# State-space outputs with swapped matmul operands, wider weight conversions and later transposes in a streaming encoder step

## The chip, the core and the metric

The kernel runs on one core of a Trainium2 chip. The metric is the device time in microseconds (us) of one execution, median over runs.

## What is computed

One layer of a hybrid encoder over 2048 new frames of one stream (16 tiles of 128 tokens) and 16 new frames of eight running streams (one more tile, number 16). All data are float32.

```python
h = _rms_norm(x, norm_gain)
u, g_s, q, k, v, g_a = jnp.split(h @ w_in, SPLITS, axis=-1)   # six groups of 512
y_s = S5(u)            # 32 groups of 16 channels, a 64-dim complex diagonal state each, scanned over positions
#   y = gelu(Re(C h) + D u);  z_val, z_gate = split(y @ w_glu);  y_s = z_val * sigmoid(z_gate)
y_a = BandAttn(q, k, v)   # 8 heads of 64, own chunk of 64 frames and the 8 before
out = x + concat[y_s * silu(g_s), y_a * silu(g_a)] @ w_out
```

## The kernel before

**Foreground and background.** The program is a fixed order of instructions that two generators write together. The foreground (`inproj`, `glu`, `outproj`) writes projections; after each step it yields a cost, and the background (`s5`, `decode`, `attention`) is given that cost times a ratio and writes its own instructions in between. A step is one k of a projection: three matmuls of 512 columns in `mm3` (high part by high weights L189, high by low weights L190, low by high weights L191). There are 1224 steps: three passes of the input projection (u and k; v and q; ga and gs) over 17 tiles, order 16, 0, 1, ..., 15, with 16 steps a tile; the GLU with 8 steps a tile; the output projection with 16. Each engine runs its instructions in that order, and SP issues nearly all DMAs in that order too. `defer(n, fn)` writes something n steps later. While weight conversions are due (`self.busy`, L1509) the ratio is 0, and the background gets nothing.

**Weights.** `load_w` (L136) loads a chunk of 128 x 512 into one of five raw buffers. `conv_w` (L142) splits it into a high part on ScalarE (L155) and a low part on VectorE (L156), 16 buffers each, and writes the load of chunk n + 5 two steps later (at once during the start). At the last tile of a pass `due` (L394) lays the next pass's 16 conversions (8 for the GLU) into the coming steps.

**Transposes of k and q.** `ev_norm` (L269) evacuates a k or q tile on ScalarE into `zs`, sums squares on VectorE (L279), takes the power on POOL (L281), scales `zs` on VectorE eight steps later (L284), and 14 steps later `turn` (L291) makes four TensorE transposes (L294), evacuates them as high (L303) and low parts (L304) and writes two stores.

**State space.** `s5` first prepares tables, then works through 8 batches of 4 channel groups. Time is cut in 272 columns (chunks of 8 tokens): 256 of the prompt, 16 of the samples. Per batch `u` is loaded, permuted and transposed into `UT` (L722), multiplied into `v` (`step_b1`, L771, 272 columns), rotated and scanned on VectorE, and gives the states `HP`. `build_e` (L698) copies a small table into `T` with eight DMAs. `step_c` (L834) makes the outputs in three blocks of 128, 128 and 16 columns, with the columns' data as the stationary operand (L842, L843; L849, L852), and GELUs them on ScalarE; `step_y` (L859) stores each block to `y_d`, token by token, in pieces of 256 bytes. The scan stage runs beside passes 1 and 2.

**GLU.** `glu_load` (L1334) loads a tile of `y`, `glu_tr` (L1339) transposes it with four TensorE instructions (L1344) into PSUM, and ScalarE (L1347) and VectorE (L1348) make the high and low parts that the GLU's matmuls use six steps later.

**Start.** Weights and the first two tiles are loaded in turn; 16 conversions are made, and `dma_h(2)` (L370) issues the third tile's `xraw` load after them.

## Time and profile before

| | us |
|---|---|
| median of 3 runs | 1225.95 |
| lowest, highest of them | 1225.14, 1464.7 |
| the profiled execution, its time | 1226.13 |
| its span in the profile | 1224.3 |
| TensorE, VectorE, ScalarE, POOL busy | 1193.0, 742.6, 597.7, 366.6 |

A row of the timeline gives start, duration, engine, line, operation, output<-inputs, shapes and count, and in brackets the engine's idle time before it with what ended it. Matmuls are pipelined: durations overlap, and the distance from start to start is the price.

### The profile page before, as it was taken

The page shows a single profiled execution, that of the slowest core. Times are in us where ns is not written, and L with a number is a line of the kernel's source. Part 1 is how long each engine was busy: PE and PEld are TensorE (multiplying, and loading weights), DVE is VectorE, ACT ScalarE, POOL GpSimd, SP SyncE. Part 2 cuts the span into 40 slices and gives each one's busy share as a digit, 9 for nine tenths or more (in the row PEclk, how much of TensorE's full clock was granted, in tenths as well). Part 3 has the DMA queues.
Part 4 walks back from the last instruction along what each step waited for, and adds up shares of the span by engine and source line. Part 5 has one row for each costly group of instructions (what it writes and reads, how often), then busy time and mean ns, then how long its engine had stood idle before and what let it go on. Part 6 is the DMA issues. An engine that isn't in the chain of part 4 may idle for free.

```text
span 1224.3 us, 18936 instructions
## 1 busy us (share of the span) xinstructions
PE 1193.0 (97%) x6687; PEld 983.1 (80%) x6687; DVE 742.6 (61%) x1391; ACT 597.7 (49%) x1159; POOL 366.6 (30%) x455
## 2 busy tenths in 40 slices
PE   8999999899999998999999999999999999999998
PEld 5788888777788876887777878788888888888876
DVE  5324556868999988985444456565565555555511
ACT  6434446266666656553232346565654555455410
POOL 2433242557767735540000011111211121121120
PEclk9999999999999998999999999999999999999999
DMA  8876556655545567433895688897877777767243
GB/s 252 262 250 181 155 177 202 195 142 129 149 123 151 135 195 214 110 93 88 270 382 171 204 247 245 255 265 205 217 221 215 206 240 241 196 205 225 73 136 107
DMA packets 190119, 236.58 MB, mean 193 GB/s; under 512 B 58136, under 2 KB 122656, under 8 KB 189000
## 3 DMA queue, kind: packets, MB, share of 16 engines
q1 hardware_dynamic: 189016, 232.15, 64.2%
q0 software_dynamic: 864, 3.21, 0.8%
q8 instruction: 53, 0.87, 0.3%
q14 instruction: 42, 0.34, 0.1%
q10 hardware_dynamic: 144, 0.00, 0.0%
HBM read 169.48 MB, written 67.80 MB: 194 GB/s over the span
## 4 chain that ended last, share of the span: by engine, by line
PE 78%; DMA 6%; DVE 6%; POOL 3%; ACT 3%; issue 2%; SPq 1%; DVEq 0%; ACTq 0%; POOLq 0%
PE z L189 19%; PE z L191 18%; PE z L190 18%; PE o L1218 6%; PE pt L1200 5%; PE s L1170 5%; DMA wraw<-in_w_in_dram 3%; PE pt L294 1%; PE o L1057 1%; PE y L843 1%; SPq L701 1%; PE y L842 1%; PE v L771 1%; ACT whi L155 1%; PE s L1015 1%
## 5 line engine op out<-in xcount | busy, mean ns | idle before, releaser
L189 PE MATMUL z<-whi,hhi 128*128 128x512 f32 x816 | 339.2, 416 | 1.4 <-ACT whi L155 0.7
L190 PE MATMUL z<-wlo,hhi 128*128 128x512 f32 x816 | 321.3, 394 | 3.3 <-DVE wlo L156 3.1
L191 PE MATMUL z<-whi,hlo 128*128 128x512 f32 x816 | 320.7, 393 | 0.5 <-DVE hlo L231 0.5
L189 PEld LDWEIGHTS z<-whi,hhi 128*128 128x128 f32 x816 | 154.1, 189 | 38.9 <-issue 5.1
L190 PEld LDWEIGHTS z<-wlo,hhi 128*128 128x128 f32 x816 | 154.5, 189 | 36.5 <-DVE wlo L156 8.0
L191 PEld LDWEIGHTS z<-whi,hlo 128*128 128x128 f32 x816 | 154.0, 189 | 34.3 <-DVE hlo L231 1.0
L1207 ACT ACTIVATE pth<-pt 128x640 fp32r<-128x640 f32 (+4 forms) x128 | 81.7, 639 | 129.3 <-PE pt L1200 89.4
L1208 DVE TENSOR_TENSOR ptl<-pt,pth 128x640 fp32r<-128x640 f32 (+4 forms) x128 | 94.6, 739 | 60.6 <-ACT pth L1207 59.7
L189 PE MATMUL z<-whi,mh 128*128 128x512 f32 x272 | 113.7, 418 | 0.0
L1115 POOL MEMSET bias<- 64x64 f32 x32 | 4.7, 146 | 363.5 <-DMA bias<-tl_d 250.0
L1189 ACT ACTIVATE sn<-sn,mn 128x640 f32<-128x640 f32 (+4 forms) x128 | 96.9, 757 | 29.5 <-DVE mn L1180 29.4
L191 PE MATMUL z<-whi,ml 128*128 128x512 f32 x272 | 107.1, 394 | 1.3 <-POOL ml L1415 1.3
L190 PE MATMUL z<-wlo,mh 128*128 128x512 f32 x272 | 106.7, 392 | 0.0
L1180 DVE CUSTOM_DVE_ANT_0 sn<-s,bias 128x640 f32<-128x640 f32 (+4 forms) x128 | 93.3, 729 | 11.4 <-PE s L1170 10.4
L1170 PE MATMUL s<-ks,q 128*128 128x320 f32 (+1 forms) x448 | 87.4, 311 | 0.0
L1200 PE MATMUL pt<-ident,sn 128*128 128x128 f32 x560 | 83.0, 274 | 3.9 <-DVE ptl L1208 3.1
L1170 PEld LDWEIGHTS s<-ks,q 128*128 128x128 f32 x448 | 74.7, 188 | 11.1 <-DVE mn L1180 1.2
L1200 PEld LDWEIGHTS pt<-ident,sn 128*128 128x128 f32 x560 | 64.9, 140 | 22.5 <-ACT sn L1189 10.0
L231 DVE TENSOR_TENSOR hlo<-xraw,hhi 128x1024 fp32r<-128x1024 f32 x49 | 60.9, 1242 | 20.7 <-ACT hhi L228 20.6
L280 POOL TENSOR_SCALAR s<-s 128x8 f32<-128x8 f32 x34 | 15.9, 468 | 182.9 <-DVE s L279 182.3
L1228 DVE TENSOR_TENSOR ot<-o,tmp 64x512 f32<-64x512 f32 x32 | 22.0, 689 | 74.5 <-ACT tmp L1226 74.5
L191 PEld LDWEIGHTS z<-whi,ml 128*128 128x128 f32 x272 | 51.0, 188 | 13.2 <-POOL ml L1415 1.7
(268 smaller groups left out, 2171.3 us busy)
## 6 DMA issues: line engine op xcount, KB each, us to landing
xraw<-in_xT_dram SPq DMA_DIRECT2D x49, 512.0 KB, 4.5
q<-qt_d SPq DMA_DIRECT2D x64, 256.0 KB, 8.6
ks<-kt_d SPq DMA_DIRECT2D x28, 512.0 KB, 5.6
vhl<-vp_d SPq DMA_DIRECT2D x28, 512.0 KB, 6.7
wraw<-in_w_in_dram SPq DMA_DIRECT2D x48, 256.0 KB, 4.5
bias<-tl_d SPq DMA_DIRECT2D x32, 320.0 KB, 6.3
mt<-mt_d SPq DMA_DIRECT2D x17, 512.0 KB, 7.4
x<-in_x_dram SPq DMA_DIRECT2D x34, 256.0 KB, 5.8
```

What stands on the lines that cost most here:

```text
L189: mm(z, a, whi, start=first, stop=False)
L190: mm(z, a, wlo, start=False, stop=False)
L191: mm(z, b, whi, start=False, stop=last)
L231: nc.vector.tensor_sub(lo, raw, fv(hi))
L1170: nc.tensor.matmul(ps_s[:, bank, 0:wp], Q[n, x2][:, s, 128 * a:128 * a + 128], KS[n][:, s, c0:c0 + wp], start=(x2 == 0), stop=(x2 == 1))
L1180: nc.vector.tensor_tensor_reduce(out=o, in0=i0, in1=i1, scale=1.0, scalar=3e38, op0=OP.add, op1=OP.min, accum_out=mn)
L1189: nc.scalar.activation(out=sn[:, 0:w], in_=sn[:, 0:w], func=AF.Exp, scale=-1.0, bias=mn, accum_out=SUM[n][:, a, s:s + 1])
L1200: nc.tensor.transpose(t[:, k], pr[:, 128 * k:128 * k + 128], self.ident)
L1207: nc.scalar.activation(out=h, in_=t[:, 0:w], func=AF.Copy)
L1208: post.append(lambda: nc.vector.tensor_tensor(out=l, in0=t[:, 0:w], in1=fv(h), op=OP.subtract))
L1218: nc.tensor.matmul(o[:, a0:a1], VB[n][:, j, s, :], t[:, 3 * a0 + j + a0:4 * (a1 - 1) + j + 1:4], start=(y == 0 and j == 4), stop=(y == 1 a ...
L1228: post.append(lambda: nc.vector.tensor_tensor(out=ot[mine], in0=o[mine], in1=tmp[mine], op=OP.add))
```

## The change

The state-space outputs are computed with the tables as the stationary operand and the data as the moving one, one group of 272 columns at a time, so that they come out with channels on partitions; the sample's columns move from the end to the front. They are stored in that form by eight DMAs a batch, in pieces of 16 elements (64 bytes). The GLU then reads its operand already transposed, with rows of `w_glu` loaded in the matching order, and its TensorE transposes go; `glu_conv` only splits into high and low parts. At the changes of pass, conversions start at step 2 instead of 4 and are 1.6 steps apart instead of 1.25 (into the GLU still 1.25). The last tile's `turn` of k and q, and tile 16's of q, come six steps later. In the start, the five raw weights of the next pass are loaded at steps 40 to 80 instead of at once, and `dma_h(2)` comes before the last four conversions instead of after them. The first `build_c` comes after one more pause.

```diff
-        self.y_d = d.tile([NT * 128, 512], F32, name="y_d")
+        self.y_d = d.tile([4, CH, 8, NT, 128], F32, name="y_d")
...
-        self.identr = c.tile([128, 128], F32R, name="ident")
-        self.ident = fv(self.identr)
-        nc.vector.tensor_scalar(self.identr, ip, 0.0, None, op0=OP.is_equal)
+        self.ident = c.tile([128, 128], F32, name="ident")
+        nc.vector.tensor_scalar(self.ident, ip, 0.0, None, op0=OP.is_equal)
...
-            self.chunks += [((3, f, k), I["w_glu"][128 * k:128 * k + 128, 512 * f:512 * f + 512], None) for k in range(4)]
+            self.chunks += [((3, f, k), I["w_glu"][128 * k:128 * k + 128, 512 * f:512 * f + 512]
+                             .rearrange("(g h) c -> h g c", h=CH), None) for k in range(4)]
...
         if self.step:
             self.defer(self.T_LW, lambda: self.load_w(n + self.NR))
+        elif n + self.NR < 16:
+            self.load_w(n + self.NR)
         else:
-            self.load_w(n + self.NR)
+            self.defer(40 + 10 * (n + self.NR - 16), lambda: self.load_w(n + self.NR))
...
-            self.defer(self.T_TURN, turn)
+            self.defer(self.T_TURN + (6 if t == 15 or (g, t) == ("q", 16) else 0), turn)
...
             for _ in range(4):
                 self.conv_w()
-        dma_h(2)
+            if j == 0:
+                dma_h(2)
...
-                    self.due(self.step + 4, 1.25, 16 if ps < 2 else 8)
+                    self.due(self.step + 2, 1.6 if ps < 2 else 1.25, 16 if ps < 2 else 8)
...
-                            self.glu_tr(TILES[0])
+                            self.glu_conv(TILES[0])
...
         BLK = [(0, 128), (128, 128), (256, 16)]
+        COL = [16, 144, 0]
...
-            nc.scalar.activation(out=UT[b][:, :, c0:c0 + n], in_=p[:, :, 0:n], func=AF.Copy)
+            nc.scalar.activation(out=UT[b][:, :, COL[i]:COL[i] + n], in_=p[:, :, 0:n], func=AF.Copy)
...
-        def step_c(b, i):
-            c0, n = BLK[i]
-            p = ps.tile([128, GB, 128], F32, tag="y", name="y", bufs=2)
-            y = mp.tile([128, L, GB * CH], F32, tag="y", name="y")
...
-                for g in range(GB):
-                    nc.tensor.matmul(p[0:n, g], UT[b][:, g, c0:c0 + n], Tm[b % 2][:, g], start=True, stop=False)
-                    nc.tensor.matmul(p[0:n, g], HP[b][:, g, c0:c0 + n], ca[g], start=False, stop=True)
-                nc.scalar.activation(out=yg, in_=p[0:n].rearrange("p g (j h) -> p g j h", j=L), func=AF.Gelu_apprx_tanh)
...
+        def step_c(b, g):
+            if g == 0:
+                YS[b] = mp.tile([128, GB, 272], F32, tag="y", name="y", bufs=1)
+            p = ps.tile([128, 272], F32, tag="y", name="y", bufs=2)
+            nc.tensor.matmul(p, Tm[b % 2][:, g], UT[b][:, g], start=True, stop=False)
+            nc.tensor.matmul(p, CA[b][:, g, 1:9].rearrange("p j h -> p (j h)"), HP[b][:, g, 0:272],
+                             start=False, stop=True)
+            nc.scalar.activation(out=YS[b][:, g], in_=p, func=AF.Gelu_apprx_tanh)
...
-        def step_y(b, i):
-            c0, n = BLK[i]
-            y = YS.pop((b, i))
-            nc.sync.dma_start(y4[c0:c0 + n, :, b * GB * CH:(b + 1) * GB * CH], y[0:n])
+        def step_y(b):
+            y = YS.pop(b)
+            o0 = (b // 2) * CH * 8 * NT * 128 + (b % 2) * 4 * NT * 128
+            for j in range(L):
+                nc.sync.dma_start(ap_of(self.y_d, o0 + 16 * j, [[8 * NT * 128, CH], [128, GB * NT], [1, 16]]),
+                                  y[16 * j:16 * j + 16].rearrange("p g (t c) -> p (g t) c", c=16))
...
             if n == 0:
+                yield SL
                 build_c(0)
...
-                if b and 1 <= sl < 4:
-                    step_y(b - 1, sl - 1)
+                if b and sl == 3:
+                    step_y(b - 1)
...
-                if b and sl < 3:
-                    step_c(b - 1, sl)
+                if b:
+                    for g in ((0,), (1,), (2, 3), (), (), ())[sl]:
+                        step_c(b - 1, g)
...
-        for i in range(3):
-            step_c(NBATCH - 1, i)
-            yield 1740
-            step_y(NBATCH - 1, i)
+        for g in range(GB):
+            step_c(NBATCH - 1, g)
+            yield 1300
+        step_y(NBATCH - 1)
...
-        self.nc.sync.dma_start(y, self.y_d[128 * t:128 * t + 128])
+        self.nc.sync.dma_start(y.rearrange("p (k x) -> p k x", k=4),
+                               self.y_d[:, :, :, (t + 1) % NT].rearrange("k h g x -> (h g) k x"))
...
-    def glu_tr(self, t):
+    def glu_conv(self, t):
         nc = self.nc
-        y = self.GY.pop(t)
-        pt = self.pst.tile([128, 4, 128], F32, tag="tr", name="ty")
-        for k in range(4):
-            nc.tensor.transpose(rv(pt[:, k]), rv(y[:, 128 * k:128 * k + 128]), self.identr)
+        y = self.GY.pop(t).rearrange("p (k j c) -> p k c j", k=4, j=L)
         hi = self.hp.tile([128, 8, 128], F32R, tag="hhi", name="yh")
         lo = self.hp.tile([128, 8, 128], F32R, tag="hlo", name="yl")
-        nc.scalar.activation(out=hi[:, 0:4], in_=pt, func=AF.Copy)
-        self.defer(1, lambda: nc.vector.tensor_tensor(out=lo[:, 0:4], in0=pt, in1=fv(hi[:, 0:4]), op=OP.subtract))
+        h4, l4 = (v[:, 0:4].rearrange("p k (c j) -> p k c j", j=L) for v in (hi, lo))
+        nc.scalar.activation(out=h4, in_=y, func=AF.Copy)
+        self.defer(1, lambda: nc.vector.tensor_tensor(out=l4, in0=y, in1=fv(h4), op=OP.subtract))
...
-                            self.glu_tr(TILES[i + 1])
-                            yield 430
+                            self.glu_conv(TILES[i + 1])
```

## Rows read from the trace of the kernel before

**Rows 1.** The page's head: busy time, share and instructions by engine.

```profile
PE 1193.0 (97%) x6687; PEld 983.1 (80%) x6687; DVE 742.6 (61%) x1391; ACT 597.7 (49%) x1159; POOL 366.6 (30%) x455
```

**Rows 2.** Timeline of TensorE at foreground's pace: start, duration, engine, line.

```profile
443.46 0.40 PE L190 MATMUL z<-wlo,hhi 128*128 128x512 f32 x1
...
453.22 0.39 PE L191 MATMUL z<-whi,hlo 128*128 128x512 f32 x1
```

**Rows 3.** By stretch: length, busy PE, PEld, DVE, ACT, POOL, clock, DMA share, GB/s.

```profile
210.00:220.00 10.00, 7.58 (x33) 5.78 (x32) 8.04 (x13) 5.10 (x8) 4.41 (x3) 0.96 0.79 237
220.00:230.00 10.00, 10.00 (x40) 8.06 (x39) 9.76 (x26) 3.10 (x5) 2.85 (x3) 0.87 0.81 253
470.00:480.00 10.00, 7.65 (x37) 5.40 (x37) 9.65 (x15) 7.13 (x18) 8.22 (x11) 0.66 0.77 242
257.00:443.00 186.00, 184.10 (x1017) 149.07 (x1017) 168.63 (x286) 114.40 (x256) 128.92 (x144) 1.00 0.52 137
```

**Rows 4.** Timeline of TensorE: output blocks of 128 and 16 columns, and L771.

```profile
298.60 0.38 PE L842 MATMUL y<-T,UT 128*128 128x128 f32 x2
...
300.62 0.39 PE L190 MATMUL z<-wlo,hhi 128*128 128x512 f32 x1
...
304.40 0.41 PE L849 MATMUL y<-T,UT 128*16 128x128 f32 x8
...
305.29 0.40 PE L190 MATMUL z<-wlo,hhi 128*128 128x512 f32 x1
...
406.50 0.62 PE L771 MATMUL v<-UT,VB 128*128 128x272 f32 x2
...
407.18 0.39 PE L190 MATMUL z<-wlo,hhi 128*128 128x512 f32 x1
```

**Rows 5.** Timeline of TensorE: GLU's transposes, once alone, once waiting.

```profile
701.93 0.46 PE L1344 MATMUL ty<-ident,y 128*128 128x128 f32 x4
...
702.53 0.40 PE L190 MATMUL z<-wlo,hhi 128*128 128x512 f32 x1
...
707.92 0.51 PE L1344 MATMUL ty<-ident,y 128*128 128x128 f32 x4 [1.35 <-DMA y<-y_d]
```

**Rows 6.** Timeline of TensorE at the change from pass 0 to 1.

```profile
218.73 0.69 PE L294 MATMUL pt<-ident,zs 128*128 128x128 f32 x4 [2.17 <-DVE zs L284]
```

**Rows 7.** Timelines of TensorE, VectorE and ScalarE at the change from 1 to 2.

```profile
472.84 1.09 PE L294 MATMUL pt<-ident,zs 128*128 128x128 f32 x4 [2.35 <-DVE zs L284]
...
468.95 2.71 DVE L156 SCALAR_TENSOR_TENSOR wlo<-wraw,gain,whi 128x512 fp32r<-128x512 f32 x3
...
457.16 2.79 ACT L155 ACTIVATE whi<-wraw,gain 128x512 fp32r<-128x512 f32 x4 [6.24 <-DMA wraw<-in_w_in_dram]
```

**Rows 8.** Timeline of TensorE in the start and at the scan's start.

```profile
35.72 0.50 PE L191 MATMUL z<-whi,hlo 128*128 128x512 f32 x1 [0.53 <-DVE hlo L231]
...
250.51 0.41 PE L686 MATMUL pk<-CA,X 128*16 128x128 f32 x8 [1.96 <-ACT UT L734]
```

**Rows 9.** DMA issues: transfer, queue, count, KB each, median us to landing.

```profile
xraw<-in_xT_dram SPq DMA_DIRECT2D x49, 512.0 KB, 4.5
...
wraw<-in_w_in_dram SPq DMA_DIRECT2D x48, 256.0 KB, 4.5
...
qbd<-qsd SPq DMA_DIRECT2D x2, 128.0 KB, 5.4
```

**Rows 10.** Groups by line: busy us, mean ns, idle us before and releaser.

```profile
L228 ACT ACTIVATE hhi<-xraw 128x1024 fp32r<-128x1024 f32 x49 | 51.8, 1056 | 4.9 <-DMA xraw<-in_xT_dram 4.9
...
L719 ACT ACTIVATE P<-U 128x512 f32<-128x512 f32 (+1 forms) x24 | 15.0, 625 | 0.1
```

**Rows 11.** Timeline of SP: eight issues in a row of T's copies.

```profile
436.28 6.17 SPq L701 DMA_DIRECT2D T<-kr  x8
```

**Rows 12.** Instructions on `qsd`: issue ns min/median/max, first and last start.

```profile
L982 SPq DMA_DIRECT2D qbd<-qsd x2: 584/2044/3503, 589.1 to 589.7; - x2
```

**Rows 13.** Instructions on `xraw`, 257 to 577: issue ns, first and last start.

```profile
L214 SPq DMA_DIRECT2D xraw<-in_xT_dram x21: 327/339/953, 267.4 to 568.4; - x21
```

More of the change, by code (lines that the diff above doesn't have):

```diff
@@ L33, in fv @@
     return ap.bitcast(F32)
-def rv(ap):
-    return ap.bitcast(F32R)
 def ap_of(t, offset, pat):
@@ L703, in s5 @@
         u4 = self.u_d.rearrange("(c j) e -> c j e", j=L)
-        y4 = self.y_d.rearrange("(c j) e -> c j e", j=L)
         BLK = [(0, 128), (128, 128), (256, 16)]
+        COL = [16, 144, 0]
         U, P, UT, HP = {}, {}, {}, {}
@@ L726, in step_a @@
                 HP[b] = mp.tile([128, GB, 273], F32, tag="HP", name="HP")
-                nc.vector.memset(HP[b][:, :, 0:1], 0.0)
-                nc.vector.tensor_copy(HP[b][:, :, 257:273].rearrange("p g (b k) -> p g b k", k=2)[:, :, :, 0],
+                nc.vector.memset(HP[b][:, :, 16:17], 0.0)
+                nc.vector.tensor_copy(HP[b][:, :, 0:16].rearrange("p g (b k) -> p g b k", k=2)[:, :, :, 0],
                                       h0[:, b * GB:(b + 1) * GB, :])
@@ L776, in step_swap @@
             vs = mp.tile([128, 256], F32, tag="vs", name="vs")
-            nc.scalar.activation(out=vs[0:64], in_=v[64:128, 0:256], func=AF.Copy)
-            nc.scalar.activation(out=vs[64:128], in_=v[0:64, 0:256], func=AF.Copy)
+            nc.scalar.activation(out=vs[0:64], in_=v[64:128, 16:272], func=AF.Copy)
+            nc.scalar.activation(out=vs[64:128], in_=v[0:64, 16:272], func=AF.Copy)
             if g == 0:
                 SV[b] = mp.tile([128, GB, 2 * NB], F32, tag="sv", name="sv")
-            nc.scalar.activation(out=SV[b][:, g], in_=v[:, 256:272], func=AF.Copy)
+            nc.scalar.activation(out=SV[b][:, g], in_=v[:, 0:16], func=AF.Copy)
             VV[b, g] = v, vs
@@ L790, in step_rot @@
             G = mp.tile([128, 256], F32, tag="G", name="G")
-            tt(t1, co, v[:, 0:256], op=OP.mult)
+            tt(t1, co, v[:, 16:272], op=OP.mult)
             tt(t2, si, vs, op=OP.mult)
@@ L810, in step_h @@
             tt(t4, si, Gs, op=OP.mult)
-            tt(HP[b][:, g, 1:257], t3, t4, op=OP.subtract)
+            tt(HP[b][:, g, 17:273], t3, t4, op=OP.subtract)
         def step_fin(b):
@@ L821, in step_fin @@
             w4 = sw.rearrange("p g (b k) -> p g b k", k=2)
-            h1 = HP[b][:, :, 257:273].rearrange("p g (b k) -> p g b k", k=2)[:, :, :, 1]
+            h1 = HP[b][:, :, 0:16].rearrange("p g (b k) -> p g b k", k=2)[:, :, :, 1]
             sh = [128, GB, NB]
@@ L831, in step_fin @@
             tt(FINs[:, :, gs].rearrange("p b g -> p g b"), x8, y8, op=OP.add)
-            nc.vector.tensor_copy(FINp[:, gs], HP[b][:, :, 256])
-        def step_c(b, i):
-            c0, n = BLK[i]
-            p = ps.tile([128, GB, 128], F32, tag="y", name="y", bufs=2)
-            y = mp.tile([128, L, GB * CH], F32, tag="y", name="y")
-            yg = y[0:n].rearrange("p j (g h) -> p g j h", g=GB)
-            ca = [CA[b][:, g, 1:9].rearrange("p j h -> p (j h)") for g in range(GB)]
-            if i < 2:
-                for g in range(GB):
-                    nc.tensor.matmul(p[0:n, g], UT[b][:, g, c0:c0 + n], Tm[b % 2][:, g], start=True, stop=False)
-                    nc.tensor.matmul(p[0:n, g], HP[b][:, g, c0:c0 + n], ca[g], start=False, stop=True)
-                nc.scalar.activation(out=yg, in_=p[0:n].rearrange("p g (j h) -> p g j h", j=L), func=AF.Gelu_apprx_tanh)
-            else:
-                o = [p[32 * g:32 * g + n, 0] for g in range(GB)]
-                for g in range(GB):
-                    nc.tensor.matmul(o[g], UT[b][:, g, c0:c0 + n], Tm[b % 2][:, g], start=True, stop=False,
-                                     tile_position=(0, 32 * g))
-                for g in range(GB):
-                    nc.tensor.matmul(o[g], HP[b][:, g, 257:257 + n], ca[g], start=False, stop=True,
-                                     tile_position=(0, 32 * g))
-                for g in range(GB):
-                    nc.scalar.activation(out=yg[:, g], in_=o[g].rearrange("p (j h) -> p j h", j=L),
-                                         func=AF.Gelu_apprx_tanh)
-            YS[b, i] = y
@@ L859, in step_y @@
-        def step_y(b, i):
-            c0, n = BLK[i]
-            y = YS.pop((b, i))
-            nc.sync.dma_start(y4[c0:c0 + n, :, b * GB * CH:(b + 1) * GB * CH], y[0:n])
+            nc.vector.tensor_copy(FINp[:, gs], HP[b][:, :, 272])
+        def step_c(b, g):
[6 more added lines that the diff above has]
+            nc.scalar.activation(out=YS[b][:, g], in_=p, func=AF.Gelu_apprx_tanh)
```

## The prediction, made before the change was built or timed

> **What bounds the kernel now.** I read the head of the page first: TensorE is busy 97% of the span, VectorE 61%, ScalarE 49% [rows 1]. So a change is worth what it takes off TensorE's in-order stream, or off the places where that stream stands still. A matmul's own duration in the timeline (0.39 us) overlaps its neighbours' and is no price. The price is the distance between starts: from 443.46 to 453.22 lie 43 intervals, 0.227 us each [rows 2]. A step of the foreground is three such matmuls, 0.68 us. The 1224 steps (51 tiles of input projection and 17 of output at 16, 17 of the GLU at 8) are 3672 matmuls, 833 us; background work and standing still share the other 390.
>
> Then the table by stretch, for the clock and for VectorE [rows 3]. The granted clock is 1.00 in the long scan stage, but 0.96 and 0.87 in the two slices from 210 to 230 and 0.66 from 470 to 480: for part of these TensorE ran at 1.2 GHz instead of 2.4. Both places are changes of pass. Last the timelines there, for what TensorE stood still for before the clock fell: 2.17 us at 218.73 [rows 6] and 2.35 us at 472.84 [rows 7], both before the four transposes of `turn`, both released by VectorE's L284 that scales `zs`. On VectorE, which is in order, L284 stands behind three weight conversions that run from 468.95 to 471.66; and ScalarE's half of a conversion had itself idled 6.24 us for a weight load [rows 7]. So the chain is load, conversion, scaling, transpose.
>
> **State-space outputs.** Before, a batch of four groups has two full blocks. Each is 16 matmul instructions: from 298.60 to the second projection matmul after it at 300.62 is 2.02 us, less one interval of 0.227, 1.79 us [rows 4]. The 16-row block takes 0.89 - 0.23 = 0.66 us [rows 4]. Eight batches: 8 x (2 x 1.79 + 0.66) = 33.9 us. After, each group has two products of 272 moving columns. That shape is there already, as L771: 0.68 - 0.227 = 0.453 us a product [rows 4]. 64 of them are 29.0 us. Saved: 4.9 us. ScalarE's GELUs become four of 272 columns a batch; it is 114.4 busy of 186 us there, so I cost that at nothing. The doubt is VectorE, 168.6 busy of 186 us in that stage [rows 3]: if it already sets the pace, the saving is 0.
>
> **GLU transposes.** Four per tile go: from 701.93 to 702.53, 0.60 - 0.227 = 0.37 us [rows 5], 17 tiles, 6.3 us. Once they also waited 1.35 us for `y` from DRAM [rows 5]. After, ScalarE waits for that load, and the product needs the result six steps later, at least 4.1 us; the 1.35 us go. The two copies that make the high and low halves now read SBUF in permuted order. ScalarE has such a copy of 128x512, L719, at 0.625 us [rows 10]; even twice that for both halves together stays under the 4.1 us of the same six steps, so I cost them at nothing. With that cover gone they would be 17 x 1.25, 21 us.
>
> **Change of pass.** Call L the first step of a pass's last tile. Conversion j moves from step L + 4 + 1.25j to L + 2 + 1.6j; its weights are first used at L + 16 + j. For j = 15 that is 26 instead of 22.75, against 31: the margin shrinks, but five raw buffers turn the other way. A chunk's buffer is refilled two steps after its conversion and wanted five conversions later: 4.25 steps (2.9 us) before, 6 steps (4.1 us) after, against 4.5 us from issue to landing [rows 9]. Before, the schedule asked for what the loads couldn't give, and the two in-order engines stood in the conversions. After, it asks for about what they give. The transposes at the change move six steps (4.1 us), past the last use of late weights; with them move two stores on SP's queue and the evacuations on ScalarE and VectorE. POOL's queue is passed by nothing new. What is late next is the last weights themselves.
>
> From 0 to 1: the 2.17 us, and for the clock 10 x (0.04 + 0.13) = 1.7 us, 3.9 in all. Between 0 and 3.9 I take 3.0, since the first conversions begin two steps, 1.4 us, earlier and VectorE has room there, 8.0 of 10 us [rows 3]. From 1 to 2: 2.35 us, and 10 x 0.34 = 3.4 us of clock, 5.75 in all. Here three refills in a row are waited for, background work is held back three steps longer (no batch is issued while conversions are pending), and TensorE may stand before the weights instead. I take 3.0, the clock's share more than the wait's.
>
> **Start and scan start.** Five weight loads of the next pass no longer stand in SP's queue ahead of the third tile's `xraw`; TensorE waited 0.53 us for its low half at 35.72 [rows 8]. I take 0.5. A later `build_c` frees the 1.96 us that the first `pk` waited for ScalarE [rows 8]: 1.9, because the pause gives TensorE projection matmuls to do.
>
> **The stores of `y`.** This is the added work. Per batch three stores of 256-byte pieces (2176) become eight of 64-byte pieces, 8 x 16 x 68 = 8704. Eight issues of small tiles in a row held SP 6.17 us [rows 11]. The trace has 64-byte pieces once, read from DRAM: two loads of 2048, issued at 589.1 and 589.7, held SP 0.58 and 3.50 us, 1.0 ns a piece, and one is known to have landed 5.4 us after its issue [rows 9, 12]. That puts 8704 at about 8.7 us; if the 5.4 us are the second's, both took 6.0 us to the landing, 1.5 ns a piece, 12.8 us. What is queued behind them on SP: `xraw`, the `kt`, `vhl` and `u` traffic. `xraw` comes every 301 / 20 = 15.05 us in the scan [rows 13], 0.94 us a step; it is issued at step 3 of a tile and wanted at step 17, 13.2 us later, less 4.5 us of landing [rows 9], so 8.7 us to spare. A burst of b us overruns that, averaged over where it falls, by (b - 8.7)^2 / (2 x 15.05): nothing at 8.7, 0.56 us at 12.8, eight times 4.5 us. I take 1 us, nearer to the issue's rate, because SP's hold is what the row shows directly.
>
> **Sum.** 4.9 + 6.3 + 1.35 + 3.0 + 3.0 + 0.5 + 1.9 - 1 = 19.95 us off the profiled execution's 1226.13 (span 1224.3, 1.8 around it): 1206. The median of the three runs is 1225.95, so the same sum holds for it.
>
> **Rivals.**
> The stores decide (slower). Place: SP's queue in the scan. If a 64-byte write to DRAM takes twice the price of that read, b is 25.6 us and each burst overruns `xraw` by 16.9^2 / 30.1 = 9.5 us, eight times 76 us: about 1283. The gain of 21 us is used up at 2.6 us a burst, b = 17.5 us, 2.0 ns a piece. For it: no row shows such a small write to DRAM. Against it: behind the eight T copies, which hold SP 6.17 us too [rows 11], `xraw` came in time: ScalarE idled for it 4.9 us in the whole run, the start included [rows 10]. The Trainium skill speaks for this rival: "DMA: Bandwidth & Descriptors", Specifications, asks for at least 512 bytes for line rate, since below that the DMA reads, modifies and writes. The old 256-byte stores were already under that size, and no row here shows what the rule would cost at 64 bytes. Chance 0.08.
>
> The wider interval gives nothing, or VectorE sets the scan's pace. The loads take as long as before, TensorE stands before the weights instead of before `turn`, and the clock falls as it did: 6 us back, 1212; if only the 4.9 us of the scan are lost, 1211. For it: 6.24 us of waiting for a load are no matter of order. Against it: from 0 to 1 VectorE is busy 8.0 of 10 us and not 9.65 [rows 3], so the earlier start counts. Chance 0.22.
>
> All waits at the changes go, and the clock stays at 2.4 GHz: the sum is 4.9 + 6.3 + 1.35 + 3.9 + 5.75 + 0.5 + 1.96 = 24.7, some small waits with it, about 1200. For it: both falls of the clock came right behind these two gaps, so the gap alone need go. Chance 0.25.
>
> **Numbers.** The forecast, 1206, has 0.45. The range takes in 1212 and 1200 with 3 to 5 us for the unknown ends (the stores' 4.5 us upward): 1196 to 1217; the slower rival is left out, and a tenth for what I don't see. 2% of 1225.95, about what can be told from no change, puts the bounds at 1201.4 and 1250.5. Faster by more: most of the last rival and the low end of the forecast, 0.27. Slower by more: most of the first, 0.06. Within: 0.67.
>
> **What would show it.** Right: no L1344; `y` products at 0.23 us between starts, 128 of them; the clock 0.95 or more in every slice of both changes of pass; `turn` with no idle behind L284. Wrong: idle of projection matmuls behind L155 or L156 around 215 and 470 as large as before; ScalarE's L228 waiting for `xraw` in the scan, or SP held over 15 us by the eight stores; a GELU waiting for the store before it, as `y` has one buffer.

## The result and the profile of the changed kernel

The changed kernel takes 1245.2 us (median of 4 runs, 1243.97 to 1247.95) against 1226.39 for the kernel before: a ratio of 1.016, 95% interval 1.014 to 1.018. It is slower by 1.6%. (The ratio leaves out the slow run of the kernel before, 1464.7 us.) The forecast was 1206 us, 1196 to 1217: wrong in size and in sign. The profiled execution took 1244.3 us, its span is 1242.1.

The page's head (busy time, share and instructions by engine):

```profile
PE 1190.8 (96%) x6363; PEld 973.1 (78%) x6363; DVE 752.4 (61%) x1391; ACT 600.5 (48%) x1143; POOL 371.4 (30%) x455
```

TensorE has 324 instructions fewer than in [rows 1], and the span is 17.8 us longer: work went, and standing still came. To find where, I count the foreground's matmuls in the traces, three to a step, and compare the time at which a step begins. The first row is the time in the kernel before; the others are the difference to it, in us.

| step | 64 | 304 | 336 | 544 | 592 | 720 | 800 | 952 | 1223 |
|---|---|---|---|---|---|---|---|---|---|
| before | 58.6 | 233.6 | 263.0 | 456.0 | 507.4 | 619.1 | 693.8 | 889.3 | 1218.6 |
| after | -1.5 | -0.6 | -3.5 | -0.4 | -0.2 | 6.8 | 13.4 | 11.5 | 18.5 |
| e1 | -1.1 | 1.7 | -1.5 | -0.3 | -4.0 | -1.2 | 5.9 | 3.3 | 6.5 |
| e2 | 5.2 | 5.2 | 5.2 | 3.9 | 0.4 | 4.7 | 4.7 | 5.0 | 13.7 |
| e3 | -1.3 | -0.2 | -3.0 | -0.3 | -2.6 | 7.3 | 13.8 | 7.1 | 14.5 |
| e4 | -2.3 | -0.4 | -3.6 | -2.0 | -1.6 | -2.5 | 4.9 | 3.1 | 10.7 |
| e5 | -1.1 | 0.2 | -3.0 | 0.6 | -1.1 | 7.3 | 16.3 | 16.5 | 18.4 |
| e6 | -1.3 | 0.9 | -2.3 | 1.3 | -0.3 | 9.1 | 15.7 | 13.2 | 21.5 |
| e7 | -1.6 | 0.0 | -2.5 | -3.4 | -8.9 | -0.9 | 3.0 | 1.2 | 9.2 |
| e8 | -0.4 | -2.1 | -1.4 | -1.4 | -2.6 | 1.7 | 3.8 | 2.5 | 8.7 |
| e9 | -1.5 | 0.8 | -1.5 | -1.2 | -6.1 | 2.9 | 6.8 | 4.7 | 12.9 |
| e10 | -0.7 | 0.5 | -2.0 | -2.7 | -8.1 | 1.8 | 5.7 | 7.2 | 9.6 |
| e11 | -0.6 | 0.7 | -2.1 | -1.6 | -7.4 | -0.5 | 3.4 | 1.9 | 10.4 |
| e12 | -1.3 | -0.2 | -2.3 | -2.0 | -7.7 | 1.4 | 5.2 | 4.0 | 11.7 |
| e13 | -0.8 | 1.6 | -0.9 | -2.2 | -8.5 | -14.9 | -2.5 | -14.1 | 6.5 |
| e14 | -1.1 | -0.1 | -2.5 | -2.9 | -8.7 | -15.3 | -5.3 | -4.6 | 7.0 |
| e15 | -0.8 | -1.6 | -2.7 | -1.6 | -7.6 | -7.1 | -3.2 | 1.1 | 3.4 |
| e16 | -0.6 | -0.6 | -1.5 | -1.0 | -7.2 | -6.3 | -1.4 | -1.7 | 1.1 |
| e17 | -1.3 | -1.9 | -2.9 | -3.4 | -9.7 | -16.0 | -3.7 | -6.8 | 3.5 |
| e18 | 5.2 | 5.7 | 5.7 | 5.3 | 5.4 | 5.4 | 5.4 | 1.8 | 0.4 |

Steps 272 to 304 are the change of pass 0 to 1, 304 on the scan, 544 to 592 the second change, 592 to 720 the end of the scan and decode's start, 816 to 952 the GLU, then the output projection. By step 592 some 12 us should have been won, and nothing was; then 13.6 us are lost up to step 800, and 7.0 behind step 952. Each row is one profiled execution. Where the background starts later, a difference at a step also holds work that was put off: behind step 592 stand 29% of the `y` products in the kernel before and 38% in the changed one.

**What the products cost.** Timeline of TensorE in the changed kernel: one group's two products between foreground matmuls.

```profile
575.87 0.62 PE L843 MATMUL y<-UT,T 128*128 128x272 f32 x2
...
577.02 0.40 PE L191 MATMUL z<-wlo,hhi 128*128 128x512 f32 x1
```

1.15 us less one interval of 0.227 is 0.92 us a group: the price read from L771 in [rows 4] holds.

**The change of pass 0 to 1.** Timeline of TensorE, then windows (length, busy PE, PEld, DVE, ACT, POOL, clock, DMA share, GB/s).

```profile
214.43 0.50 PE L191 MATMUL z<-wlo,hhi 128*128 128x512 f32 x1 [1.43 <-DVE wlo L154]
218.61 0.50 PE L191 MATMUL z<-wlo,hhi 128*128 128x512 f32 x1 [1.83 <-DVE wlo L154]
```

```profile
210.00:220.00 10.00, 6.74 (x26) 4.22 (x25) 8.52 (x12) 4.49 (x7) 4.39 (x3) 0.95 0.84 264
220.00:230.00 10.00, 10.00 (x41) 8.16 (x42) 9.79 (x27) 3.60 (x5) 2.92 (x2) 0.88 0.68 217
```

The 2.17 us in front of `turn` [rows 6] are gone; 1.43 and 1.83 us in front of late weights stand in their place, and the clock is as in [rows 3].

**The scan.** Timeline of TensorE, and the slice 280 to 290, once more from the changed kernel.

```profile
279.32 0.66 PE L737 MATMUL ut<-ident,P 128*128 128x128 f32 x4 [2.58 <-ACT VB L682]
308.92 0.70 PE L775 MATMUL v<-UT,VB 128*128 128x272 f32 x2 [2.13 <-DVE t L795]
```

```profile
280.00:290.00 10.00, 10.00 (x48) 7.74 (x48) 9.51 (x17) 4.36 (x11) 8.17 (x9) 0.83 0.67 166
```

In the kernel before, TensorE's longest wait from 257 to 443 is 1.29 us (`ut` for `VB`, at 313.42), and the clock is 1.00 [rows 3].

**A store in SP's queue.** Timelines of SP, ScalarE and TensorE in the scan.

```profile
386.69 8.79 SPq L853 DMA_DIRECT2D y_d<-y  x8
395.52 1.14 SPq L245 DMA_DIRECT2D qt_d<-kt  x1
```

```profile
400.04 0.69 ACT L304 ACTIVATE kt<-pt,qg 128x512 fp32r<-128x512 f32 x1 [6.29 <-DMA qt_d<-kt]
```

```profile
401.77 0.66 PE L737 MATMUL ut<-ident,P 128*128 128x128 f32 x4 [1.75 <-ACT kr L698]
```

The eight stores hold SP 8.79 us. Behind them stands the store of `kt`, which has one buffer; ScalarE waits 6.29 us to write the next `kt`, `kr` waits behind that on ScalarE, and TensorE for `kr`. This wait for a late store of `kt` stands in the changed kernel, e3, e5 and e6, and in no other run.

**The last batch's stores.** Timelines of SP, VectorE and TensorE at the end of the scan, and the slice behind it.

```profile
586.35 9.00 SPq L853 DMA_DIRECT2D y_d<-y  x8
595.76 0.67 SPq L926 DMA_DIRECT2D out_dram<-of  x1
```

```profile
598.32 0.29 DVE L933 COPY of<-pf 128x128 f32<-128x128 f32 x1 [7.47 <-DMA out_dram<-of]
598.66 0.47 PE L931 MATMUL pf<-ident,FINs 128*128 128x128 f32 x1 [4.54 <-DVE of L933]
```

```profile
600.00:610.00 10.00, 10.00 (x35) 8.00 (x35) 4.51 (x8) 0.69 (x1) 0.95 (x1) 0.76 0.47 135
```

The small stores of the final states stand 9 us behind the eight; their one buffer `of` holds VectorE 7.47 us, and TensorE 4.54. Then the clock is 0.76 for ten microseconds, 1.00 in the same slice before: part of them at 1.2 GHz.

**The GLU.** Groups by line (busy us, mean ns, idle before): the two copies in the kernel before, in the changed kernel and in e3, an experiment below.

```profile
L1347 ACT ACTIVATE yh<-ty 128x512 fp32r<-128x512 f32 x17 | 10.2, 597 | 9.5 <-PE ty L1344 9.4
L1348 DVE TENSOR_TENSOR yl<-ty,yh 128x512 fp32r<-128x512 f32 x17 | 11.7, 688 | 5.5 <-ACT yh L1347 5.3
```

```profile
L1341 ACT ACTIVATE yh<-y 128x512 fp32r<-128x512 f32 x17 | 18.6, 1094 | 4.3 <-DMA y<-y_d 4.2
L1342 DVE TENSOR_TENSOR yl<-y,yh 128x512 fp32r<-128x512 f32 x17 | 20.3, 1196 | 16.4 <-ACT yh L1341 16.1 <-DMA ga_d<-plain 0.3
```

```profile
L1341 ACT ACTIVATE yh<-y 128x512 fp32r<-128x512 f32 x17 | 10.6, 623 | 5.3 <-DMA y<-y_d 5.2
L1342 DVE TENSOR_TENSOR yl<-y,yh 128x512 fp32r<-128x512 f32 x17 | 12.9, 758 | 11.7 <-ACT yh L1341 11.7
```

A few long copies raise VectorE's means; its medians are 686, 1055 and 692 ns.

TensorE's waits from 715 to 960 (us in total, times, longest): before, after, and e3.

```profile
PE pt L1200 <- DVE ptl L1208: 2.7, 5, 0.9
```

```profile
PE pt L1194 <- DVE ptl L1202: 10.3, 13, 1.7
```

```profile
PE pt L1194 <- DVE ptl L1202: 6.1, 9, 1.4
```

### The profile page after: what moved, and what is told of

It is laid out like the page before. It is cut to its first block, busy times and chain, and to the rows that moved or that the text cites. A ratio compares the mean times of both kernels' runs of the same rounds, so it can differ in the third digit from the quotient of the medians.

```text
span 1242.1 us, 18278 instructions
## 1 busy us (share of the span) xinstructions
PE 1190.8 (96%) x6363; PEld 973.1 (78%) x6363; DVE 752.4 (61%) x1391; ACT 600.5 (48%) x1143; POOL 371.4 (30%) x455
## 4 chain that ended last, share of the span: by engine, by line
PE 61%; DVE 8%; DMA 4%; ACT 4%; issue 3%; SPq 3%; DVEq 0%; ACTq 0%
PE z L190 13%; PE z L192 13%; PE z L191 13%; PE o L1212 6%; PE pt L1194 5%; PE s L1164 5%; SPq L853 1%; DMA wraw<-in_w_in_dram 1%; PE y L844 1%; PE v L775 1%; PE y L843 1%; DVE ptl L1202 1%; DVE hlo L232 1%; ACT yh L1341 1%; DMA qt_d<-kt 1%
## 5 line engine op out<-in xcount | busy, mean ns | idle before, releaser
L190 PE MATMUL z<-whi,hhi 128*128 128x512 f32 x816 | 344.0, 422 | 1.3 <-ACT zs L276 0.6
L325 ACT ACTIVATE th<-z,hrstd 128x512 f32<-128x512 f32 x34 | 23.4, 688 | 83.1 <-PE z L192 58.5
```

The lines of the kernel that those rows point to most:

```text
L190: mm(z, a, whi, start=first, stop=False)
L325: nc.scalar.activation(out=th, in_=z, func=AF.Tanh, scale=h)
```

## The experiments

Ratios are to runs of the kernel before on the same chip in the same batch (its medians there: 1226.0 to 1228.0).

| | median us | ratio, 95% interval |
|---|---|---|
| e1 timing edits alone | 1233.63 | 1.007, 1.005 to 1.009 |
| e2 y path alone | 1240.07 | 1.012, 1.009 to 1.015 |
| e3 split unpermuted | 1244.76 | 1.015, 1.011 to 1.019 |
| e4 one store a batch | 1236.58 | 1.009, 1.006 to 1.013 |
| e5 pause back in the GLU | 1243.27 | 1.013, 1.009 to 1.017 |
| e6 pf before stores | 1247.44 | 1.017, 1.014 to 1.020 |
| e7 no extra pause | 1234.28 | 1.006, 1.004 to 1.009 |
| e8 old change of pass | 1232.42 | 1.003, 1.001 to 1.005 |
| e9 = e6 + e7 | 1237.35 | 1.008, 1.006 to 1.010 |
| e10 = e9 + GLU mended | 1237.47 | 1.008, 1.007 to 1.010 |
| e11 pause compensated | 1238.16 | 1.009, 1.006 to 1.011 |
| e12 = e9, stores spread | 1237.39 | 1.008, 1.006 to 1.010 |
| e13 = e9, last stores spaced | 1234.36 | 1.005, 1.003 to 1.007 |
| e14 = e13 + GLU mended | 1230.53 | 1.003, 1.001 to 1.004 |
| e15 = e1 without the pause | 1229.1 | 1.001, 0.999 to 1.003 |
| e16 = e15, ms on VectorE | 1226.56 | 0.999, 0.997 to 1.000 |
| e17 = e14, ms on VectorE | 1228.25 | 1.001, 0.999 to 1.002 |
| e18 = before, one GLU transpose | 1225.59 | 0.998, 0.997 to 1.000 |

**The two halves.** e1 is the kernel before with the edits of `load_w`, `dma_h`, `due`, `turn` and the extra pause; e2 the changed kernel without them.

> The kernel before with only the timing edits: deferred raw loads and the earlier xraw load in the start, the extra pause ahead of the first build_c, conversions at step 2 with 1.6 between, the transposes of the last tile six steps later. State-space outputs, their stores and the GLU are as before. Theory 'stores and copies' (the losses come with the new y path): the start's 1.5 us, the 2.0 us of the first pk and some 2 us at the changes of pass stay, and 1219 to 1222 us come out. Rival 'order' (the later background and the later conversions put VectorE's and ScalarE's work of the scan beside other work of the foreground): the waits of v at 306 and 478 and the clock's fall at 280 to 290 are there without the new y path too, and the time is 1225 to 1232 us.

> The new y path alone (swapped operands, eight stores of 64-byte pieces a batch, GLU without transposes), every timing edit taken back. Theory 'stores and copies': 5 us less product work and 6 us fewer transposes are met by 10 us of waiting in the GLU stage and 7 us behind the last batch's stores: 1231 to 1240 us. Rival 'order': the new path keeps most of its own gain, 1216 to 1224 us, and the loss comes with the timing edits.

Each half loses alone, 0.7% and 1.2%; e1's time lies above the ranges of both theories, e2's at the top of the first one's. Both are half right. The wait of `ut` in the scan (2.58 us) is there in e1 without the new y path; but `v` waits only 0.53 us at 309.75 and 1.21 at 479.06, and the clock is 1.00 from 280 to 290. e2 loses 5.2 us by step 64, where none of the y path runs yet (the last section has this wait), 4.3 us from step 592 to 720 behind the stores, and 9.0 from 800 to the end. In the scan it wins 4.8 us, from 5.2 to 0.4 between steps 336 and 592. Only 1.3 of them come before step 544. The other 3.5 come at the second change of pass, where the clock is 1.00 from 470 to 480 in e2 and 0.66 before [rows 3]; by the prediction's reckoning that alone is 3.4 us.

**Parts of the y path.** e3:

```diff
-        y = self.GY.pop(t).rearrange("p (k j c) -> p k c j", k=4, j=L)
+        y = self.GY.pop(t).rearrange("p (k x) -> p k x", k=4)
```

> The changed kernel, but the two splits of y in the GLU read the loaded tile in the order in which it lies, without the permutation of tokens within a chunk of eight (so the GLU works on tokens in another order: this part of the computation is changed). Number and size of all instructions stay. Theory 'copies': yh and yl fall from 1.09 and 1.20 us to about 0.60 and 0.69, the waits of pt for ptl in the GLU stage fall back, and the time is 8 to 11 us below the changed kernel, 1234 to 1237 us. Rival 'the stage is paced by attention on its own, whose work was only moved' : yh and yl get shorter and the time stays within 3 us of the changed kernel's, 1242 to 1247.

The copies fall to 623 and 758 ns, the waits of `pt` from 10.3 to 6.1 us, and steps 800 to 952 win 6.7 us instead of 1.9. The median moves only 0.4 us, though, and lies in the rival's range: its runs spread from 1240.3 to 1247.3 and the profiled one is the lowest. Shown for the stage, not for the whole.

e4:

```diff
-            for j in range(L):
-                nc.sync.dma_start(ap_of(self.y_d, o0 + 16 * j, [[8 * NT * 128, CH], [128, GB * NT], [1, 16]]), ...)
+            nc.sync.dma_start(ap_of(self.y_d, b * 128 * GB * 272, [[GB * 272, 128], [1, GB * 272]]), ...)
```

> The changed kernel with one store a batch of 128 pieces of 4352 bytes in place of eight stores of 1088 pieces of 64 bytes each; the bytes are the same, but they go to other places in y_d (so the GLU reads y in a wrong layout: this part of the computation is changed). Theory 'the stores hold SP': the wait of pf behind the last batch's stores (4.5 us) goes with the clock's fall behind it (3.4 us), and the scan's waits behind late loads and stores go too: 1231 to 1236 us. Rival 'the scan is late by VectorE and the order': only the end of the scan gets better, 1236 to 1240 us, and the scan's lost time stays.

8.6 us less, in the rival's range, and the place is nearly the rival's too: from step 592 to 720 the difference goes from +7.0 to -0.9, while the scan up to 592 wins 1.4 us. From 720 to 800 nothing is won: 7.4 us are lost there with one store as well, 6.6 in the changed kernel. Issues on `y_d` (ns min/median/max, first and last start), changed kernel and e4:

```profile
L853 SPq DMA_DIRECT2D y_d<-y x64: 318/966/2825, 316.0 to 594.6; - x64
```

```profile
L852 SPq DMA_DIRECT2D y_d<-y x8: 319/382/1053, 314.8 to 584.1; - x8
```

e5 puts `yield 430` back behind `glu_conv`.

> The changed kernel with the pause of 430 put back into the GLU, behind each tile's split (the change took it away together with the transposes). Theory 'moved work': without the pause 9 us less of attention's TensorE work is written into the GLU stage and has to be done in the output stage, where TensorE has no idle time; with it back the output stage (steps 952 to 1160) falls from 294 us to about 286 and the time to 1236 to 1240 us. Rival 'the GLU stage is paced by the chain pt, pth, ptl': what the output stage wins the GLU stage loses, and the time stays within 3 us of the changed kernel's, 1242 to 1247.

The time is in the rival's range, and what the output stage wins is larger than what the GLU loses. Steps 952 to the end lose 1.9 us instead of 7.0, but steps 800 to 952 lose 0.2 where 1.9 were won: moved work, of which 3 us is net; the profiled execution lost as much at step 592 to 800 as it won here.

e6 writes `pf`, `of` and their stores ahead of the last `step_y`.

> The changed kernel with the final states (pf, of and their small output stores) written ahead of the last batch's eight stores of y instead of behind them. Theory 'the stores hold SP': the 4.5 us in which the second pf waited for of go, the clock's fall behind them (3.4 us) too, 1236 to 1239 us. Rival 'pf would wait anyway': the time stays at 1242 to 1246, and another wait stands at that place.

The rival holds; the time is even 1.4 us above its range. `pf` no longer waits; `xs` (2.08 us) and decode's first `s` (2.12 us) do, and the clock falls from 610 to 630.

**Parts of the timing.** e7 takes out the extra `yield SL`; e8 puts back `due(self.step + 4, 1.25, ...)` and `turn`'s old delay.

> The changed kernel without the extra pause ahead of the first build_c. Theory 'order': the pause puts the whole scan five steps later against the foreground; without it the first pk waits about 2 us for ScalarE again, but the 2.6 us before ut at 276 (VB late on ScalarE) go with the clock's fall at 280 to 290, and the later ones change: 1238 to 1243 us. Rival: the pause brings its 2 us and the scan's waits are the stores' alone: 1246 to 1248.

> The changed kernel with the conversions and the last tile's transposes at the changes of pass as before. Theory 'order': the new spacing gives nothing at the first change, wins about 3 us up to the end of the second change and gives them back in the next 16 steps, where background work that was held back for four steps longer comes at once, and decode comes earlier again: 1240 to 1244 us. Rival 'the wider interval works': 1248 to 1251.

Both win 11 to 13 us, much more than either theory expected. The scan's first `v` comes at step 330 in the kernel before and at 335 in the changed one: the trace gives three of these steps to the conversions, during which the background gets nothing, and two to the pause (not five, as I wrote for e7). It starts at 333 in e7 and 332 in e8. The slice that fell to 0.83 is whole in e7 (it is whole in e1, e4, e5 and e6 too, which start at 335; in e4 to e6 the slice from 310 to 320 falls instead, to 0.83 to 0.88):

```profile
280.00:290.00 10.00, 9.80 (x55) 7.25 (x54) 9.51 (x17) 5.29 (x12) 7.64 (x8) 1.00 0.57 160
```

e8 wins its time elsewhere: 1.2 us from step 336 to 592, but from 592 to 800 it loses 6.4 us and not 13.6. Its clock at the second change is 0.67, as before.

**The pause or the shift.** e11 keeps the pause and drops the one behind `build_e(0)`, so that the scan starts at 333 again; e9 is e6 and e7 together.

> The changed kernel with the extra pause ahead of the first build_c, and the pause behind build_e of the first batch taken out, so that the scan starts at the same step as without the extra pause. Theory 'it is the shift of the scan by five steps, not the pause' : the first pk finds ScalarE ready (its 2 us go) and the scan goes as in e7, 1231 to 1235 us. Rival 'it is what stands at that place' (build_c, later feeds, the order of the first batch): the waits at 266 to 280 and 306 stay, 1241 to 1246 us.

> The changed kernel without the extra pause and with the final states written ahead of the last batch's stores (e6 and e7 together). In e7 the kernel was 9.6 us ahead of the kernel before at step 592, and the second pf then waited 8.0 us for of. Theory 'the pause's shift and the stores' hold of SP are two causes': the 8 us and the clock's fall behind them go, 1222 to 1226 us. Rival 'another wait follows' (as in e6, where xs, a decode product and the clock took the place of pf): 1231 to 1236 us.

In e11 steps 336 to 592 win 5.3 us, as in e7 (6.4): up to there it is the shift, though e11's time lies between the ranges of both theories. Of the kernels with the new y path and the new change of pass, those whose scan starts at 335 (after, e3 to e6) lose 0.4 to 3.3 us there, those at 333 (e7, e9 to e14, e17) win 4.6 to 7.6. With the old y path the same two steps cost 3.6 us by step 592 (e1 against e15). The loss from step 720 to 800 follows the start too, whatever the y path: 0.0 us at 330 (e2, e18), 2.1 at 332 (e8), 3.8 to 4.9 at 333 (e7, e9 to e12, e15, e16), 6.5 to 9.0 at 335 (the changed kernel, e1, e3 to e6). The stores are not its cause, since e1 has the old ones; what is, no run separates.

In e11 and e7 the gain of the scan is then lost to a longer wait of `pf` (7.9 and 8.0 us). e9, whose time is 1.4 us above its rival's range, loses it elsewhere. Timeline of VectorE in e9:

```profile
596.67 0.22 DVE L979 TENSOR_REDUCE m<-ident 128x1 f32<-128x64 f32 x1 [9.52 <-DMA y_d<-y]
...
611.45 0.69 DVE L327 SCALAR_TENSOR_TENSOR plain<-th,xs 128x512 f32<-128x512 f32 x1 [10.97 <-DMA gs_d<-plain]
```

Decode's first tile lies in the memory that the stored `y` held, so VectorE waits 9.52 us for the stores to land; then a foreground store stands behind decode's loads on SP, 10.97 us. From step 592 to 720 the burst costs about the same three times, by three waits: 7.0 us in the changed kernel, 9.4 in e6, 9.0 in e9.

**Spread stores.** e12 is e9 with the stores in pairs at four places of the scan; e13 spaces the last batch's too and frees their memory later:

```diff
+        for j in range(0, L, 2):
+            yield 1000
+            step_y(NBATCH - 1, range(j, j + 2))
+        yield 3000
```

> e9 with the eight stores of y of a batch spread in pairs over four places of the scan, instead of eight in a row. Theory 'the stores hold SP in the scan too' (kt's one buffer waited 6.3 us for its store behind them, ut 1.8 us behind that): 2 to 4 us less than e9. Rival 'only the last burst mattered': within 1.5 us of e9.

> e9 with the last batch's eight stores in pairs, 1000 of pause ahead of each pair, and 3000 behind the last before the state space's memory is given free for decode. Theory 'the last burst costs some 10 us wherever it stands, through SP's order and through VectorE, which waits for the stores' landing before it may write decode's first tile into that memory': no wait of more than 1 us from step 592 to 752, the clock stays at 1.00 there, and the time is 9 to 11 us below e9: 1226 to 1229 us. Rival 'decode, which now comes some 18 steps later, collides elsewhere': 1232 to 1238 us.

e12 equals e9, as the rival has it: inside the scan of e9, where the wait behind `kt` is gone already, the burst cost little. e13's time is in its rival's range. It goes from -8.5 at step 592 to -14.9 at 720, partly because decode now starts at step 733 instead of 715; that comes back by step 800. From 592 to 800 it loses 6.0 us, e9 12.9, and e15 below, which has none of these stores, 4.4: most of the burst's cost is gone. But attention, which starts 15 steps later, is then done in the output stage, and the end is only 3 us better.

**The GLU mended.** e10 (on e9) and e14 (on e13) split `y` in the order in which it lies, load `gs` by rows in that order, turn `ms` with an identity of permuted columns, and have the pause back.

```diff
+        nc.gpsimd.tensor_copy(idp.rearrange("p (c j) -> p j c", j=L), self.ident.rearrange("p (j c) -> p j c", j=L))
...
-                nc.tensor.transpose(pt[:, k], ms[:, 128 * k:128 * k + 128], self.ident)
+                nc.tensor.transpose(pt[:, k], ms[:, 128 * k:128 * k + 128], idp)
...
-            nc.sync.dma_start(g, self.gs_d[128 * t:128 * t + 128])
+            nc.sync.dma_start(g, self.gs_d[128 * t:128 * t + 128].rearrange("(c j) e -> j c e", j=L))
```

> e9 with the GLU mended: the split reads y in the order in which it lies, the tokens of the GLU stay in that order, gs is loaded by rows in the same order, and the transposes of ms use an identity with permuted columns, so that mt comes out right; and the pause of 430 is back. Theory 'copies and pause cost the GLU its gain': yh and yl take 0.60 and 0.69 us again, and steps 800 to 1160 take 5 to 8 us less than in e9: 1215 to 1221 us. Rival 'the GLU stage is paced by attention's chain': within 3 us of e9.

> e13 with e10's GLU (y split in the order in which it lies, gs by rows in that order, permuted identity for ms, the pause of 430 back). Theory 'copies and pause cost the GLU its gain': steps 800 to the end take 3 to 7 us less than in e13, and the time is 1220 to 1225 us, below the kernel before. Rival 'attention's chain paces the GLU': within 2 us of e13.

e10 equals e9, as the rival has it. e14 is 3.8 us better than e13 by the medians, as much as the first theory has it, but above its range and not below the kernel before. Nor is the place shown: in the two profiled executions (1232.71 and 1232.12 us) steps 800 to the end take 3.3 us more in e14 than in e13. In both, new waits stand at the GLU's start: 4.0 us of attention's `s` for VectorE at 720.84 in e10, 5.1 us of `tm` for POOL at 720.31 in e14.

**The timing without the pause, and POOL's order.** e15 is e1 without the pause. In it, and in e9 to e14, the transposes `tm` wait for POOL. PE's waits in e15 from 690 to 960; then POOL and SP in e9:

```profile
PE tm L1364 <- POOL ms L1405: 4.5, 1, 4.5
```

```profile
736.92 0.15 POOL L1108 MEMSET bias<- 64x64 f32 x1 [12.72 <-DMA bias<-tl_d]
737.12 0.14 POOL L1109 MEMSET bias<- 64x64 f32 x1
737.23 1.26 POOL L1392 TENSOR_TENSOR ms<-ms,gs 128x512 f32<-128x512 f32 x1
```

```profile
733.64 0.92 SPq L1107 DMA_DIRECT2D bias<-tl_d  x1
```

POOL writes a corner of attention's bias and has to wait for the load that SP issued late; the GLU's product stands behind it. e16 and e17 put that product on VectorE for the first eight tiles.

> The kernel before with the timing edits but without the extra pause ahead of build_c; outputs, stores and GLU as before. Theory 'the pause did the harm in e1': the start's 1.5 us and about 3 us at the changes of pass are kept, decode four steps later takes 2 us of them: 1221 to 1225 us. Rival 'the conversions' longer stretch does the harm': 1228 to 1234 us, as e1.

> e15 with the product of ms and gs of the GLU's first eight tiles on VectorE instead of POOL. In e15 the transposes of ms waited 4.5 us for that product at 725: POOL, in order, stood before a small write into an attention bias that had not landed. Theory 'POOL's order': that wait goes with the clock's fall behind it (1.7 us): 1222 to 1225 us, below the kernel before. Rival 'VectorE has no room there': another wait of the same size, 1227 to 1231 us.

> e14 with the same edit. There five such waits took 10.8 us, and the clock fell in three slices between 710 and 820 (5.1 us). Theory 'POOL's order': 1216 to 1222 us, and steps 800 to 952 take some 10 us less than in the kernel before. Rival 'VectorE has no room there': 1227 to 1232 us.

e15: without the pause 4.5 us of e1's median go, and step 592 comes at -7.6 against -4.0: most of e1's harm was the pause's. The time is in the rival's range all the same, because 4.3 us go between 800 and 952 although the GLU is the old one. In e16 these steps win 0.3; its median is 2.5 us below e15's, between its two ranges. e17's is 2.3 us below e14's, in the rival's range. The intervals of each pair overlap. No version that computes the whole layer beats the kernel before by what can be told.

**The transposes alone.** e18 leaves one of the four GLU transposes in the kernel before and lets both copies read it four times.

```diff
-        for k in range(4):
-            nc.tensor.transpose(rv(pt[:, k]), rv(y[:, 128 * k:128 * k + 128]), self.identr)
+        nc.tensor.transpose(rv(pt[:, 0]), rv(y[:, 0:128]), self.identr)
+        p4 = pt[:, 0:1].to_broadcast([128, 4, 128])
```

> The kernel before with one of the four GLU transposes of a tile left in and three taken out; the two copies read the one result four times over, so they stay as large as before (the GLU works on a quarter of y: this part of the computation is left out). 51 transposes of 0.092 us, 4.7 us of TensorE, are gone, and nothing else is changed. Theory 'TensorE's order sets the GLU stage', on which the forecast's 6.3 us rested: 1222 to 1223 us. Rival 'the stage stands as long for attention's copies': TensorE's waits in steps 816 to 952 grow by what was taken, 1226 to 1229 us.

From step 800 to 952 the trace wins 3.6 us of 4.7, to the end 5.0; by the ratio of 0.998 it is 2.3 us, 0.2 to 4.3, and the time lies between the two ranges. So such work keeps some of its price when nothing else changes: nearly all by the trace, half by the medians.

## Why the prediction was wrong, step by step

Four steps failed: the copies of the GLU priced at nothing, a pause priced only where it stands, the stores priced at 1 us, and the saved TensorE work taken as saved time.

**State-space outputs, -4.9: the price right, the gain not seen.** A group costs 0.92 us, as summed. But the prediction took the whole saving as time, and on top of the new timing next to none of it comes: step 592 is at -7.6 and -7.2 without the new path (e15, e16), at -6.1 to -9.7 with it (e7, e9 to e14, e17), 8.1 in the mean. In e2 only 1.3 us of the 4.8 stand apart from the second change of pass and its clock. The doubt that the prediction named, that VectorE sets the pace (167.7 us busy from 257 to 443 in the changed kernel, 168.6 before), is not refuted, and not shown either.

**GLU, -7.65: wrong, two steps.** "I cost them at nothing" was said of the copies, with L719 at 0.625 us [rows 10] as their price and six steps as their cover. They took 1.09 and 1.20 us in the mean, and the cover was the wrong question: both engines run attention there, whose `pt`, `pth`, `ptl` chain TensorE waits for, 10.3 us instead of 2.7. L719 was no model: in `glu_conv` neighbours that are read one after the other lie 64 bytes apart, and with neighbours side by side (e3) the same copies took 0.62 and 0.76. The Trainium skill, "SBUF — State Buffer", Door 1, states that consecutive accesses to the same 16-byte line run at full bandwidth and that each access which crosses to a new line pays a penalty. The trace agrees: 1.09 us against 0.62 on ScalarE. The second step is one I left out: the removed `yield 430` is attention's share of the stage. 5.1 us of the 7.0 lost behind step 952 go when it is back, 3 net. Both are shown for the stages where they stand, not for the whole time: e3's median moves 0.4 us, e10's not at all, and from step 800 to the end e10, with both mended, still loses 3.9 us (e9 6.1). The transposes' own price fits e18's trace (3.6 to 5.0 us of 4.7), and its median only by half.

**Change of pass 0 to 1, -3.0: wrong.** The idle time moved from `turn` to `wlo` L154, as the rival "the wider interval gives nothing" had it; steps 272 to 304 lost 0.9 us.

**Change 1 to 2, -3.0: right in e15, undone in the changed kernel.** In e15 the wait moved to late weights (`wlo`, 1.05 and 1.54 us) and the clock's fall went (1.00 from 470 to 480), as the forecast weighed them. Steps 544 to 592 win 6.0 us in e15, with the largest value at 5.75, and lose 0.2 in the changed kernel. (Not all of the 6.0 is the change's: e2, with the old one, wins 3.5 there, and e15 has 48 `y` instructions there instead of 64, the rest put off.) In the changed kernel `v` waits 2.05 us for VectorE right behind the change, and the clock is 0.83 from 480 to 490.

**Start -0.5: right** (-1.5 by step 64).

**build_c -1.9: wrong.** The wait of the first `pk` is gone in the changed kernel, and it is 0.69 us in e7, which has no extra pause:

```profile
250.63 0.41 PE L689 MATMUL pk<-CA,X 128*16 128x128 f32 x8 [0.69 <-ACT UT L738]
```

So most of the 1.96 us went with the other timing edits (0.69 us in e15 too, 1.96 in e2); the 2.9 us won from step 304 to 336 are 2.5 in e7. And a pause was costed only at its place. Two more steps on top of the conversions' three start the whole scan later, and by e7 and e11 that cost 7 to 9 us up to step 592. With the stores this is the largest single error. That each batch then stands beside other foreground work is the likely reason; no run shows it. Which two steps hurt isn't a rule: at 333 the gain up to 592 stays and at 335 it goes, but e8, at 332 with the old change of pass, has 1.2 us of the 4.8 that e2 has at 330.

**Stores, +1: wrong.** SP's hold was right (7.3 to 9.5 us a burst; I said 8.7). What stands behind was not `xraw` but single buffers, `kt` and `of`, and, once these were out of the way, decode's memory. I weighed the one deep-buffered load and none of the single-buffered stores. Measured: 8.6 us (e4), nearly all behind the last batch. The rival "the stores decide" had the right queue and the wrong price.

**What stays open.** In e17 TensorE's work is 15 us less than before and its standing still 18 us more, if each kind of matmul is counted at the distance to the next start that a quarter of its kind keep, and the rest of each distance as standing still. Part may be attention's later start; how the rest divides between VectorE, ScalarE and SP's order I can't tell. So with the pause out, the last stores spaced, the GLU mended and the product moved the time is that of the kernel before again; why the gains of the sum do not come then is open.

## What to carry to other kernels

In a program whose order is written by hand, a pause or a held-back background is priced by what it shifts, not by where it stands: try neighbouring shifts before judging the edit that brought it. For a burst on an in-order queue list each single-buffered tile whose store stands behind it, and who next writes the memory that it reads. An edit that takes work off the busiest engine and puts 0.5 us on two others is priced by the chain those two carry.

## What the runs showed of the hardware

- In the changed kernel's packet records 64-byte pieces took 11 ns each at the median and 256-byte ones 18 ns. The issue took 0.97 us of SP for 1088 pieces against 0.38 us for 128 pieces of 4352 bytes. Which of the two sets a burst's time is not separated: in the one at 386.69 the last piece ended at 398.38, 2.9 us behind SP's last issue.
- With the old order of loads in the start, the third tile's `xraw` landed late in two of three profiles: in e2 and e18 step 64 came 5.2 us later than in the kernel before; in none of the 17 profiles with the new order. ScalarE in e2:

```profile
36.23 1.06 ACT L226 ACTIVATE hhi<-xraw 128x1024 fp32r<-128x1024 f32 x1 [6.45 <-DMA xraw<-in_xT_dram]
```
